# One by one instead of by threes: how the gate matmuls are dealt among the work of attention

## The chip, the cores and the metric

The kernel runs on one core of a Trainium2 chip. The metric is the device time of one execution in microseconds; of several executions the median is given. TensorE (PE) multiplies matrices and accumulates the products in banks of PSUM, VectorE (DVE), ScalarE (ACT) and GpSimd (POOL) work on tiles in SBUF and PSUM, and SyncE (SP) issues most of the DMAs.

## The reference

One layer of a decoder with two token mixers side by side, for 1024 tokens of width 1024, in float32:

```python
h = rmsnorm(x, norm_mix)
(q, kc, vc, ks, vs, kw, vw, nsa_g, rq, rk, rv, rg, gate_a, gate_b) = jnp.split(h @ w_in, offsets, axis=-1)
...                                        # rotary on q, the keys and the retention's q, k
nsa_out = nsa(q, kc, vc, ks, vs, kw, vw, nsa_g, ...)   # 8 heads: compressed + selected + window attention
ret_out = silu(rg) * retention(rq, rk, rv)             # 4 heads of 128, chunks of 128
mix = sigmoid(gate_a) * (nsa_out @ w_proj_a) + sigmoid(gate_b) * (ret_out @ w_proj_b)
x = x + mix @ w_out
h = rmsnorm(x, norm_mlp)
x = x + square(relu(h @ w_up)) @ w_down
return rmsnorm(x, norm_final)
```

The case is about `gate_a` and `gate_b`, the merge gates: two products of the normed input (1024 tokens by 1024) with 1024 x 1024 of weights each, which nobody needs before the two mixers are merged. A query block of 128 tokens selects up to 16 blocks of 64 keys; with 1024 tokens that is all of them, so the selected branch of the kernel runs over all keys up to the query block.

## The kernel before

**Precision.** Every float32 product is made of three: each operand is split into a high part (a cast to the type that TensorE takes, on ScalarE) and a low part (the difference, on VectorE), and high x high, high x low and low x high are accumulated in one PSUM bank. The names end in h and l: `bh`, `bl` are the normed input, `wh`, `wl` a block of weights, `ph`, `pl` the transposed probabilities, `QQ`, `ql` the queries. Nearly all matmuls go through the helper `mm`, so that most rows of TensorE in the profile carry line 156; they are told apart by the tile they write.

**Stages.** From 0 to some 361 us into the profiled execution the input is normed and projected and retention runs; from 362 to 754 us attention; then what is left of the gates and the two mixing projections, the output projection, and the MLP up and down. The stage of the change is attention.

**Attention.** It has 32 units: 8 query blocks (7 down to 0) by 2 key groups by 2 pairs of heads. The selected and the window branch have up to 1024 and 640 keys, the compressed branch 64. A unit has two parts. `scores` multiplies queries by keys into banks `S` (pool `psS`, four banks); VectorE adds the mask there and takes the minimum of the negated scores into `mx` (lines 1008 and 1013), ScalarE makes the exponentials `pS` and `pW` from them (line 1017), VectorE the factors `cf` of sums and head gates (lines 1021 and 1022), and GpSimd scales the exponentials by these (line 1029); it also clears a part of `pW` at the start (line 982). `pv` transposes the probabilities on TensorE into banks `pt` (pool `psT`, two banks; lines 1064 and 1065), ScalarE casts them to `ph` (line 1066), VectorE takes the low part `pl` (line 1067), and TensorE multiplies by the values into `O` (pool `psO`, one bank). Every second unit `prep_q` transposes new queries `qt` into a `pt` bank (line 952) and splits them (lines 955 and 956).

**Gates.** There are 32 of them: 8 blocks of 128 columns of each of the two matrices, by 2 halves of the tokens. `gate_pieces(n)` issues gate n: 24 matmuls of 128x512 that accumulate in one PSUM tile `gps`, then a tanh on ScalarE from that tile into `gst` (line 920), and a DMA on SP's queue that stores it (line 921). The tile comes from pool `psO` and has one buffer, so the first matmul of gate n + 1 must wait until the tanh of gate n has read it; from n = 15 on (`GALT`) odd gates take one of the `S` banks instead. The weights of the next gate are loaded and split ahead (`gate_w`; lines 185 and 186). `gate_pieces` is a generator: at each `yield` it stops and the caller goes on with other work. It yields after every third matmul, so that a gate has 8 pieces, the last of which has the tanh and the store.

**The order.** For TensorE the order of instructions is that in which the code issues them (`tc.manual_schedule`); on VectorE, ScalarE and GpSimd a scheduler orders them. Attention gives each piece of work a time in units: `place(it, n, lo, hi)` puts n steps of a generator at even distances between lo and hi,

```python
        def place(it, n, lo, hi):
            for k in range(n):
                todo.append((lo + (hi - lo) * (k + 0.5) / n, len(todo), it))
```

and the list `todo`, sorted by time, is gone through once. Unit n's scores stand from n - 1 + 0.08 to n - 1 + 0.6, its `pv` from n to n + 1.05. Between n - 1 and n stand `GATES[n]` pieces of gates: 16, then 8 in each of 16 units, 6 in each of 12, 7 in each of 4, which is 244 of all 256. The 12 that are left run after attention, in one row (36 matmuls).

Of the kernel before, what the change touches and what calls it, by code (L numbers as in the profile page):

```python
# [109 lines left out]
def hybrid_block(ctx: ExitStack, tc: tile.TileContext, a: dict, out: bass.AP):  # L110
# [44 lines left out]
    def mm(o, w, m, start, stop):  # L155
        T.matmul(o, w, m, start=start, stop=stop)  # L156
# [62 lines left out]
    with ExitStack() as es:  # L219
# [474 lines left out]
        with ExitStack() as e2:  # L694
# [157 lines left out]
            for j in range(NT):  # L852
# [7 lines left out]
                n = tmp.tile([P, 512], F32, name="n", bufs=4)[:, :256]  # L860
# [13 lines left out]
            for i, j in enumerate(reversed(range(NT))):  # L874
# [6 lines left out]
                n = tmp.tile([P, 512], F32, name="n", bufs=4)  # L881
# [15 lines left out]
    def gate_w(i):  # L897
        if i < 16 and i not in gw:
            src, ii = ("w_ga", i) if i < 8 else ("w_gb", i - 8)
            gw[i] = split_w(a[src][:, ii], (KD, P), pool=wring, part=512)  # L900

    def gate_pieces(n):
        pool = gpool["p"]
        i, th = divmod(n, 2)
        dst, ii = (ga_scr, i) if i < 8 else (gb_scr, i - 8)
        ts = slice(th * 512, (th + 1) * 512)
        gate_w(i)
        gate_w(i + 1)
        h, l = gw[i]
        if n % 2 and n >= GALT and gpool["alt"] is not None:  # L910
            ps = gpool["alt"].tile([P, 512], F32, name="gps", tag="S")
        else:
            ps = pool.tile([P, 512], F32, name="gps", bufs=1)
        parts = [(h, k, x) for k in range(KD) for x in (bh, bl)] + [(l, k, bh) for k in range(KD)]
        for m, (w, k, x) in enumerate(parts):
            mm(ps, w[:, k * P:(k + 1) * P], x[:, k, ts], m == 0, m == len(parts) - 1)
            if m % 3 == 2 and m < len(parts) - 1:
                yield
        o = gsp.tile([P, 512], F32, name="gst")
        A.activation(o, ps, AF.Tanh, scale=0.5)  # L920
        nc.sync.dma_start(dst[ii, :, th], o)
        yield
# [3 lines left out]
    def all_gates():  # L926
        for n in range(32):
            yield from gate_pieces(n)

    gate_it = all_gates()  # L930
# [5 lines left out]
    with ExitStack() as e3:  # L936
# [12 lines left out]
        def prep_q(qb, g):  # L949
            tp = psT.tile([P, 4, P], F32, name="pt", tag="pt")  # L950
            for h in range(4):
                T.transpose(tp[:, h], qs[qb, g][:, h], ident)
            QQ = at.tile([P, 4, P], F32R, name="QQ")
            ql = at.tile([P, 4, P], F32R, name="ql")
            A.activation(QQ, tp, AF.Copy)
            V.tensor_sub(ql, tp, QQ)
            qs[qb, g] = (QQ, ql)
            nxt = 2 * (7 - qb) + g + 2
            if nxt < 16:
                load_q(7 - nxt // 2, nxt % 2)  # L960
            yield
# [139 lines left out]
# [3 lines that stand above are left out]
# [10 lines left out]
            place(it, n_pv(qb) - 1, n, n + 1 + V_END)  # L1114
            place(it, 1, n + 1 + V_LAST, n + 1 + V_LAST)
        for n, k in enumerate(GATES):
            place(gate_it, k, n - 1, n)
        next(prep_q(7, 0))
        for ev in sorted(todo, key=lambda v: v[:2]):
            if len(ev) > 3:  # L1120
# [580 lines left out]
```

## Time and profile before

| what | value |
|---|---|
| runs | 1568.26, 1564.6 and 1562.92 us; median 1564.6 |
| the profiled execution | 1563.77 us, of which 1562.0 are the span of its instructions |
| granted TensorE clock | 0.999 on the mean |
| TensorE busy in attention (362 to 754 us) | 385.84 of 392.00 us, 2385 matmuls and transposes |
| TensorE busy outside it | 1156.40 of 1170.0 us |

Times are microseconds from the start of the span. A row of the timeline gives an instruction's start and its length, and in brackets the idle time ahead of it on its engine and what ended that. The lengths of matmuls overlap, since a matmul's start doesn't wait for the end of the one ahead of it, so a matmul's share of the time is the distance between starts. Busy time is given by engine; PEld is the loading of weights into TensorE, beside the matmuls. In the list of waits a row names the waiting operation, the releasing one, and then total us, times and the longest.

### The profile page before, as it was taken

Reading aid. Unit: us, or ns where it says so; the run is one execution under the profiler, and the core shown is the slowest. Engines: PE = TensorE matmul, PEld = TensorE weight load, DVE = VectorE, ACT = ScalarE, POOL = GpSimd, SP = SyncE. Lnnn points to the kernel's source line nnn. Section 1 sums busy time; section 2 is a strip of 40 time slices with the busy share of each in tenths; the row PEclk is TensorE's granted clock in tenths of the full one; section 3 lists DMA queues with packets and bytes.
Section 4 is the critical chain, followed back from the end, with each engine's and each line's share of the span. In section 5 each row is a group of like instructions: output and inputs, shape, how many; then the busy total and the mean of one; then the engine's idle time right before and its main releaser. Section 6 shows DMA issues by size and latency. Waiting matters only on the chain.

```text
span 1562.0 us, 22775 instructions
## 1 busy us (share of the span) xinstructions
PE 1542.2 (99%) x7845; PEld 1293.8 (83%) x7845; DVE 1080.8 (69%) x2237; ACT 730.9 (47%) x1657; POOL 423.6 (27%) x516
## 2 busy tenths in 40 slices
PE   9999999999999999999999999999999999999997
PEld 7788888988888888888888888888888888888886
DVE  6875663765777777776765379877777667876673
ACT  6663553764677776766522234222222244443452
POOL 3120010002333333333000001744455446521320
PEclk9999999999999999999999999999999999999999
DMA  6202111342111112121644332544444597764472
GB/s 227 68 18 65 58 32 26 112 152 78 48 35 55 48 35 61 43 68 55 198 147 153 109 112 91 188 149 152 158 156 148 185 381 242 219 210 124 148 271 87
DMA packets 98900, 191.85 MB, mean 123 GB/s; under 512 B 26632, under 2 KB 30096, under 8 KB 98784
## 3 DMA queue, kind: packets, MB, share of 16 engines
q1 hardware_dynamic: 97008, 185.82, 36.2%
q0 software_dynamic: 944, 2.93, 0.5%
q10 hardware_dynamic: 832, 1.64, 0.3%
q8 instruction: 62, 1.02, 0.3%
q14 instruction: 54, 0.44, 0.1%
HBM read 140.02 MB, written 50.33 MB: 122 GB/s over the span
## 4 chain that ended last, share of the span: by engine, by line
PE 86%; DVE 6%; ACT 3%; issue 2%; POOL 0%; DMA 0%; POOLq 0%; ACTq 0%; DVEq 0%
PE mmu L156 23%; PE mm L156 20%; PE mmd L156 19%; PE gps L156 9%; PE S L156 4%; PE O L156 4%; PE pt L1065 2%; PE pt L1064 2%; ACT pW L1017 1%; PE pO L156 1%; DVE pl L1067 1%; PE pc L156 1%; DVE S L1008 1%; ACT pS L1017 0%; ACT ph L1066 0%
## 5 line engine op out<-in xcount | busy, mean ns | idle before, releaser
L1217 DVE TENSOR_TENSOR wl<-raw,wh 128x1024 fp32r<-128x1024 f32 x121 | 183.7, 1543 | 67.3 <-ACT wh L1216 66.0
L1216 ACT ACTIVATE wh<-raw 128x1024 fp32r<-128x1024 f32 x121 | 125.1, 1056 | 205.4 <-PE mmd L156 127.7
L156 PE MATMUL mmd<-wh 128*128 128x512 f32 x448 | 174.3, 389 | 0.0
L156 PE MATMUL mmd<-wl,wh 128*128 128x512 f32 x448 | 174.3, 389 | 0.0
L156 PE MATMUL mmd<-wh,wl 128*128 128x512 f32 x448 | 174.3, 389 | 0.0
L156 PE MATMUL mm<-wh,bh 128*128 128x512 f32 (+1 forms) x416 | 160.9, 390 | 1.6 <-ACT bh L271 1.0
L156 PE MATMUL mm<-wh,bl 128*128 128x512 f32 (+1 forms) x416 | 155.0, 376 | 0.0
L156 PE MATMUL mm<-wl,bh 128*128 128x512 f32 (+1 forms) x416 | 154.3, 375 | 0.0
L1067 DVE TENSOR_TENSOR pl<-pt,ph 128x512 fp32r<-128x512 f32 (+1 forms) x160 | 103.8, 649 | 35.9 <-ACT ph L1066 33.4
L1066 ACT ACTIVATE ph<-pt 128x512 fp32r<-128x512 f32 (+1 forms) x160 | 90.3, 568 | 55.2 <-PE pt L1065 54.3
L1029 POOL TENSOR_SCALAR pS<-pS,cf 128x512 f32<-128x512 f32 (+7 forms) x80 | 54.6, 688 | 225.7 <-ACT ph L1066 73.8
L1008 DVE CUSTOM_DVE_ANT_0 S<-S,edge_m 128x512 f32<-128x512 f32 (+3 forms) x192 | 100.8, 530 | 13.8 <-PE S L156 11.2
L156 PE MATMUL gps<-bl,wh 128*128 128x512 f32 x256 | 104.1, 407 | 0.0
L156 PE MATMUL gps<-bh,wh 128*128 128x512 f32 x256 | 103.1, 403 | 0.5 <-ACT gst L920 0.5
L1298 POOL TENSOR_TENSOR sf<-raw 128x512 f32<-128x512 f32 x14 | 22.9, 1633 | 294.2 <-DVE wl L1217 294.2
L156 PE MATMUL mmu<-bh,wh 128*128 128x512 f32 x256 | 99.7, 389 | 0.0
L156 PE MATMUL mmu<-bh,wl 128*128 128x512 f32 x256 | 99.6, 389 | 0.0
L156 PE MATMUL mmu<-bl,wh 128*128 128x512 f32 x256 | 99.6, 389 | 0.0
L156 PEld LDWEIGHTS mmd<-wh,wl 128*128 128x128 f32 x448 | 84.1, 188 | 17.6
L156 PEld LDWEIGHTS mmd<-wh 128*128 128x128 f32 x448 | 84.1, 188 | 17.5
L156 PEld LDWEIGHTS mmd<-wl,wh 128*128 128x128 f32 x448 | 84.1, 188 | 17.3
L156 PEld LDWEIGHTS mm<-wh,bl 128*128 128x128 f32 x416 | 78.1, 188 | 15.4 <-DVE bl L286 0.4
(362 smaller groups left out, 4033.9 us busy)
## 6 DMA issues: line engine op xcount, KB each, us to landing
raw<-u_scr SPq DMA_DIRECT2D x56, 512.0 KB, 3.9
raw<-w_down SPq DMA_DIRECT2D x41, 512.0 KB, 4.8
raw<-w_up SPq DMA_DIRECT2D x32, 512.0 KB, 3.6
u_scr<-u SPq DMA_DIRECT2D x59, 256.0 KB, 2.2
u_scr<-s SPq DMA_DIRECT2D x42, 256.0 KB, 2.0
y<-w_down SPq DMA_DIRECT2D x14, 512.0 KB, 8.3
x<-x SPq DMA_DIRECT2D x8, 512.0 KB, 5.6
qt<-q_scr SPq DMA_DIRECT2D x32, 128.0 KB, 2.4
```

The lines of the kernel that those rows point to most:

```text
L156: T.matmul(o, w, m, start=start, stop=stop)
L1008: V.tensor_tensor_reduce(sc, sc, mk, -0.125, BIGPOS, OP.add, OP.min, mx[:, b:b + 1])
L1017: A.activation(o, sc, AF.Exp, bias=mx[:, m:m + 1], scale=-1.0, accum_out=sums[:, b:b + 1])
L1029: G.tensor_scalar(v, v, cf[:, b:b + 1], 1.0, op0=OP.mult, op1=OP.mult)
L1064: T.transpose(tp[:, bi * 2], p0, ident)
L1065: T.transpose(tp[:, bi * 2 + 1], p1, ident)
L1066: A.activation(ph[:, :n], tp[:, :n], AF.Copy)
L1067: V.tensor_sub(pl[:, :n], tp[:, :n], ph[:, :n])
L1216: A.activation(h[:, :n], r, AF.Copy)
L1217: V.tensor_sub(l[:, :n], r, h[:, :n])
L1298: eng.tensor_tensor(F[:, 1], x11, x21, op=OP.subtract)
```

## The change

The generator yields after each matmul instead of each third, and three times as many steps are placed in each unit. A gate so has 24 pieces; the last still holds the last matmul, the tanh and the store. The numbers in `GATES` stay, and so does the number of gate matmuls in each unit.

```diff
--- before.py
+++ after.py
@@ -914,7 +914,7 @@
         parts = [(h, k, x) for k in range(KD) for x in (bh, bl)] + [(l, k, bh) for k in range(KD)]
         for m, (w, k, x) in enumerate(parts):
             mm(ps, w[:, k * P:(k + 1) * P], x[:, k, ts], m == 0, m == len(parts) - 1)
-            if m % 3 == 2 and m < len(parts) - 1:
+            if m < len(parts) - 1:
                 yield
         o = gsp.tile([P, 512], F32, name="gst")
         A.activation(o, ps, AF.Tanh, scale=0.5)
@@ -1114,7 +1114,7 @@
             place(it, n_pv(qb) - 1, n, n + 1 + V_END)
             place(it, 1, n + 1 + V_LAST, n + 1 + V_LAST)
         for n, k in enumerate(GATES):
-            place(gate_it, k, n - 1, n)
+            place(gate_it, 3 * k, n - 1, n)
         next(prep_q(7, 0))
         for ev in sorted(todo, key=lambda v: v[:2]):
             if len(ev) > 3:
```

In TensorE's order all other instructions keep their sequence. The gates' matmuls stood in 230 unbroken runs and stand in 439 now. Of the rows of VectorE, ScalarE and GpSimd some change places too; the order of SP's queue is the same.

TensorE at the end of gate 6, before (`gps_5258` is gate 6, `gps_5463` gate 7; the numbers at the names are counters, and differ a little between the two kernels):

```order
L156 MATMUL gps_5258<-bh_92,wl_4838 128x512 x3
L156 MATMUL O_5232<-pl_5397,Vw_2774 64x256
L156 MATMUL O_5232<-ph_5396,Vw_2774 128x256
L156 MATMUL O_5232<-pl_5397,Vw_2774 64x256
L156 MATMUL O_5232<-ph_5396,Vw_2774 128x256
L1064 MATMUL pt_5448<-ident_98,pS_5265 128x128
L1065 MATMUL pt_5448<-ident_98,pS_5338 128x128
L1064 MATMUL pt_5448<-ident_98,pS_5265 128x128
L1065 MATMUL pt_5448<-ident_98,pS_5338 128x128
L156 MATMUL O_5232<-pl_5416,Vc_2776 64x256
L156 MATMUL O_5232<-ph_5415,Vc_2776 128x256
L156 MATMUL gps_5463<-bh_92,wh_4837 128x512
```

And the same place after the change (`gps_5240` is gate 6, `gps_5447` gate 7):

```order
L156 MATMUL gps_5240<-bh_92,wl_4820 128x512 x2
L156 MATMUL O_5242<-pl_5398,Vw_2774 64x256
L156 MATMUL O_5242<-ph_5397,Vw_2774 128x256
L156 MATMUL O_5242<-pl_5398,Vw_2774 64x256
L156 MATMUL O_5242<-ph_5397,Vw_2774 128x256
L156 MATMUL gps_5447<-bh_92,wh_4819 128x512
L1064 MATMUL pt_5450<-ident_98,pS_5265 128x128
```

The first matmul of the next gate stood behind four transposes and two more multiplications by values, and stands ahead of the transposes now.

TensorE in the unit of gate 4, where the scores of a new head begin, before:

```order
L156 MATMUL S_4866<-KKs_2771,QQ_4599 128x512
L156 MATMUL S_4866<-KKs_2771,ql_4600 128x512
L156 MATMUL gps_4843<-bl_93,wh_4423 128x512
L156 MATMUL gps_4843<-bh_92,wh_4423 128x512
L156 MATMUL gps_4843<-bl_93,wh_4423 128x512
```

And after:

```order
L156 MATMUL gps_4825<-bl_93,wh_4413 128x512
L156 MATMUL S_4867<-KKs_2771,QQ_4600 128x512
L156 MATMUL S_4867<-KKs_2771,ql_4601 128x512
L156 MATMUL gps_4825<-bh_92,wh_4413 128x512
L1064 MATMUL pt_4875<-ident_98,pS_4645 128x128
```

Three gate matmuls stood in a row behind the scores; now one stands ahead of two scores and one behind them.

VectorE in the same unit, before (`mx_4921` is the minimum over one head's scores, `pl` a low part of probabilities that is taken out of a `pt` bank):

```order
L1008 ISA mx_4921 128x1
L1067 TENSOR_TENSOR pl_4950<-pt_4948,ph_4949 128x512
L1013 TENSOR_TENSOR mx_4921<-mx_4921 128x1
L1067 TENSOR_TENSOR pl_4982<-pt_4980,ph_4981 128x512
L1021 TENSOR_TENSOR sums_4920<-sums_4920 128x2
```

And after:

```order
L1008 ISA mx_4921 128x1
L1013 TENSOR_TENSOR mx_4921<-mx_4921 128x1
L1067 TENSOR_TENSOR pl_4951<-pt_4949,ph_4950 128x512
L1021 TENSOR_TENSOR sums_4920<-sums_4920 128x2
L1022 RECIPROCAL cf_4922<-sums_4920 128x3
```

The second operation on the minimum stood behind a low part, and stands ahead of it now.

## The prediction

> **What bounds the kernel now.** I read the page first, then windows over attention, then the waits of TensorE in that stretch, then single gate ends in the timeline. From the page: busy time, granted clock by slice, and the chain that ended last.
>
> ```profile
> span 1562.0 us, 22775 instructions
> PE 1542.2 (99%) x7845; PEld 1293.8 (83%) x7845; DVE 1080.8 (69%) x2237; ACT 730.9 (47%) x1657; POOL 423.6 (27%) x516
> ...
> PEclk9999999999999999999999999999999999999999
> ...
> PE 86%; DVE 6%; ACT 3%; issue 2%; POOL 0%; DMA 0%; POOLq 0%; ACTq 0%; DVEq 0%
> ```
>
> TensorE (PE) is the bound: it leads the chain with 86%, and its clock stands at full in every slice. The window of attention, and then all that PE waited for in it (total us, times, longest):
>
> ```profile
> 362.00:754.00 392.00, 385.84 (x2385) 331.19 (x2384) 287.08 (x1009) 267.63 (x787) 127.92 (x268) 1.00 0.17 52
> ```
>
> ```profile
> PE pt L1065 <- POOL pS L1029: 1.7, 4, 1.0
> PE S L156 <- ACT pS L1017: 1.3, 2, 0.9
> PE O L156 <- DVE pl L1067: 0.8, 2, 0.4
> PE pt L952 <- DVE pl L1067: 0.7, 1, 0.7
> PE S L156 <- DVE ql L956: 0.6, 2, 0.4
> PE gps L156 <- ACT gst L920: 0.5, 2, 0.2
> PE S L156 <- ACT QQ L955: 0.4, 1, 0.4
> ```
>
> In 392 us PE is busy for 385.84 and waits 6.0 us in 14 places. A better order of the same matmuls can win these 6.0 us and no more; a worse one has no floor. The sixth row is the place to watch: a gate's first matmul waits for ScalarE's tanh (gst), because gates 0 to 14 all accumulate in one PSUM bank. (From gate 15 odd gates use a scores' bank, so nothing waits so.)
>
> How long that bank needs from one gate to the next is seen where it already waits, at the end of gate 1 (PE and ACT, start and length):
>
> ```profile
> 377.37 0.39 PE L156 MATMUL gps<-bh,wl 128*128 128x512 f32 x1
> ...
> 377.80 0.60 ACT L920 ACTIVATE gst<-gps 128x512 f32<-128x512 f32 x1 [0.66 <-PE gps L156]
> ...
> 378.45 0.50 PE L156 MATMUL gps<-bh,wh 128*128 128x512 f32 x1 [0.25 <-ACT gst L920]
> ```
>
> From the start of the last matmul to the start of the next gate's first pass 1.08 us, with ScalarE idle and ready: 0.39 for the matmul to end, 0.6 of tanh, the rest handover. At other gate ends that time is filled. The end of gate 13:
>
> ```profile
> 556.12 0.39 PE L156 MATMUL gps<-bh,wl 128*128 128x512 f32 x1
> 556.35 0.28 PE L156 MATMUL O<-pl,Vw 128*64 128x256 f32 x1
> ...
> 556.54 0.60 ACT L920 ACTIVATE gst<-gps 128x512 f32<-128x512 f32 x1
> ...
> 556.83 0.27 PE L1064 MATMUL pt<-ident,pS 128*128 128x128 f32 x1
> ...
> 557.18 0.36 PE L156 MATMUL O<-pl,Vw 128*64 128x256 f32 x1
> ...
> 557.74 0.40 PE L156 MATMUL gps<-bh,wh 128*128 128x512 f32 x1
> ```
>
> Between the two gates stand four O matmuls (556.35 to 556.83, 0.48 us), four transposes (to 557.26 at 0.11 each), and four more O: 1.62 us, which covers the 1.08.
>
> **The change part by part.** No instruction is added or removed. In the order of PE all matmuls but the gates' stand in the same sequence as before; ahead of any of them the count of gate matmuls differs by one at most. What moves is where each gate matmul stands, and with it a few rows of DVE and ACT.
>
> *1. The gate's end.* The first pair of orders above: the next gate's first matmul now stands ahead of the transposes. It waits for the tanh there, and everything behind it on PE waits too. The cover that is left is the four O. This holds at the ends of gates 2 to 13, twelve times. Cost where ScalarE is ready: 1.08 less the matmul's own 0.23 and the 0.48 of O, 0.37 us. Eight ends (2, 4, 6, 8, 10 to 13) are such: 3.0 us. At gate 1 the four transposes leave the gap altogether: 0.44 us more. At gate 0 nothing changes.
>
> At the ends of gates 3, 5, 7 and 9 ScalarE is late; gate 7:
>
> ```profile
> 470.95 0.64 ACT L185 ACTIVATE wh<-raw 128x512 fp32r<-128x512 f32 x1
> ...
> 471.47 0.61 ACT L920 ACTIVATE gst<-gps 128x512 f32<-128x512 f32 x1
> 471.66 0.33 PE L1065 MATMUL pt<-ident,pS 128*128 128x128 f32 x1 [0.23 <-POOL pS L1029]
> ...
> 472.28 0.40 PE L156 MATMUL gps<-bh,wh 128*128 128x512 f32 x1
> ```
>
> A weight split (wh) stands ahead of the tanh, which ends at 472.08. The next gate would start at 472.13, and its matmul (0.23), four transposes (0.44) and two O (0.23) would be through at 473.03. Before, all that and one gate matmul were through at 472.28 + 0.24 = 472.52. So 0.5 us, less than the wait itself, since the transposes' wait for GpSimd falls inside it. Gate 9 alike. At gates 3 and 5 an O waits for DVE in the old order; gate 5:
>
> ```profile
> 440.80 0.61 ACT L920 ACTIVATE gst<-gps 128x512 f32<-128x512 f32 x1
> ```
>
> ```profile
> 441.70 0.33 PE L156 MATMUL O<-pl,Vw 128*64 128x256 f32 x1 [0.38 <-DVE pl L1067]
> ...
> 442.22 0.40 PE L156 MATMUL gps<-bh,wh 128*128 128x512 f32 x1
> 442.46 0.39 PE L156 MATMUL gps<-bl,wh 128*128 128x512 f32 x1
> ```
>
> The tanh ends at 441.41, so the gate matmul, four transposes and four O (0.47) would be through at 441.46 + 0.23 + 0.44 + 0.47 = 442.60, against 442.46: 0.14, and gate 3 near it, 0.2. Together 1.3. Part 1 is 3.0 + 0.44 + 1.3 = **+4.7 us**. Ends: 3.0 if the late four cost nothing and gate 1 neither; 12 x (0.37 + 0.6) + 0.44 = 12.1 if ScalarE comes a split late at all twelve.
>
> *2. More runs.* The matmuls of the gates stand in 230 unbroken runs before and in 439 now. A run of eight is timed where gates stand alone, a run of three among attention's work:
>
> ```profile
> 754.17 1.98 PE L156 MATMUL gps<-bh,wl 128*128 128x512 f32 x8
> 755.99 0.39 PE L156 MATMUL gps<-bh,wh 128*128 128x512 f32 x1
> ```
>
> ```profile
> 376.92 0.85 PE L156 MATMUL gps<-bh,wl 128*128 128x512 f32 x3
> ...
> 377.61 0.27 PE L1064 MATMUL pt<-ident,pS 128*128 128x128 f32 x1
> ```
>
> Eight take 755.99 - 754.17 = 1.82 us, 0.227 each; three take 0.69, 0.23 each, so 0.01 us over for the run. If all of it belongs to breaking a run, 209 more runs cost 2.1 us; if it belongs to company, nothing. I take the middle, **+1.0 us**. [...]
>
> *3. The waits inside units.* With one gate matmul more ahead of it, a late instruction waits 0.23 us less; the second pair of orders shows one such shift, by which one gate matmul stands ahead of two scores (S) and one behind, where three stood behind. The three long waits among the four below each get one more ahead, and so do the two late waits for GpSimd at the end of the stage; the last row below gets one less.
>
> ```profile
> 392.03 0.44 PE L952 MATMUL pt<-ident,qt 128*128 128x128 f32 x2 [0.73 <-DVE pl L1067]
> ```
>
> ```profile
> 576.06 0.36 PE L156 MATMUL S<-KKw,QQ 128*128 128x192 f32 x1 [0.89 <-ACT pS L1017]
> ```
>
> ```profile
> 674.52 0.33 PE L1065 MATMUL pt<-ident,pS 128*128 128x128 f32 x1 [1.02 <-POOL pS L1029]
> ```
>
> ```profile
> 581.61 0.36 PE L156 MATMUL S<-KKw,QQ 128*128 128x192 f32 x1 [0.45 <-ACT pS L1017]
> ```
>
> Five gains less one loss, 4 x 0.23 = 0.9, and 0.4 for waits under 0.2 us that go with them: **-1.3 us**. Ends: -5.5 (all rows of the list but gst) and 0.
>
> *4. DVE and ACT.* The third pair of orders: on DVE the minimum over a head's scores (mx) stood behind a copy out of PSUM (pl), and now stands ahead of it. The exponentials that wait for mx can start a copy earlier, and in exchange one cast (ph) stands behind them on ACT. This comes in the units of gates 3 to 9. I take 0: earlier exponentials make the tanh no later, a later cast makes it so. Ends, by one cast of 0.6 us either way in seven units: -4.2 and +4.2. SP's queue holds the same rows in the same order; each gate's store goes out with its tanh, and no one waits for it in this stage. GpSimd's clears (MEMSET) shift by one scaling; it is busy 127.92 of 392 us, so I cost them at nothing.
>
> Sum: 4.7 + 1.0 - 1.3 + 0 = +4.4 us. On the profiled execution's 1563.8 us (span 1562.0) that gives **1568.2 us**; the median of the three runs shown, 1564.6, is 0.8 above that execution.
>
> **The rivals.** *Dearer gate ends (slower).* If ScalarE comes late at all twelve ends, part 1 is 12.1 and the time 1575.6. For it: part 4 pushes a cast towards the tanh. Against: at eight ends ScalarE is idle or just done when the gate ends. It decides from 0.6 us of delay. 0.10.
>
> *The finer order pays (faster).* If the one gate matmul between S and S keeps PE busy through all waits of the list, and the gate ends hide, 5.5 us go and 1.0 comes: 1559.3. It needs the tanh within the 0.71 us of one matmul and four O; the rows show 1.08. 0.06.
>
> *Nothing moves.* If DVE and GpSimd, given the idle at the gate ends, are never waited for afterwards, the gains there (up to 5.5) meet the 5.7 of parts 1 and 2: 1564.0. For it: at gates 3, 5, 7 and 9 the old waits do fall into the new one. Against: the three longest stand far from any end of gates 2 to 13, or ahead of it. 0.07.
>
> *The clock falls.* More short stops on PE could lower its clock. [...] Here the window with 14 stops stands at 1.00, so 0.01. The eight warm-up matmuls at the start took 3.59 us against 1.98 for the eight gates above; one unit of 392/32 = 12.2 us at that pace costs 12.2 x (3.59/1.98 - 1) = 9.9 us: 1578.
>
> ```profile
> 1.48 3.59 PE L156 MATMUL pS<-warm 128*128 128x512 bf16 x8 [1.48 <-DVE warm L442]
> ```
>
> **How the numbers follow.** My case has 0.76. A measurement of this kernel tells a change from none beyond about 0.3%, 4.7 us. My sum is just under that, so the case splits, 0.42 within and 0.34 slower. With the rivals: same 0.42 + 0.07 + 0.01 of the faster one = 0.50; slower 0.34 + 0.10 + 0.01 = 0.45; faster 0.05. The range reaches down to the rival in which nothing moves, 1564, and up to where half of the delays of the dear case come, 1573; outside lie the far half of that case, the clock and the faster rival.
>
> **What would show it.** Right: the row "PE gps <- ACT gst" grows from 2 times to about 14, and from 0.5 us to some 4 to 6, with the next gate's first matmul 1.08 us or more after the last; "PE pt <- POOL pS" shrinks; windows outside attention stay. Wrong: that row stays at 2, or rows with S, pt or O grow instead.

## The result, and the profile after

The changed kernel takes 1576.02 us (median of four runs, 1575.84 to 1576.95), the kernel before 1563.80 in the same comparison: a ratio of 1.0077, with a 95% interval of 1.0064 to 1.009. It is 12.2 us slower, outside the range forecast (1564 to 1573).

From the page of the profile after: the span, busy times, the clock by slice, and the chain that ended last.

```profile
span 1574.0 us, 22755 instructions
PE 1547.3 (98%) x7845; PEld 1291.5 (82%) x7845; DVE 1088.9 (69%) x2237; ACT 731.2 (46%) x1657; POOL 422.2 (27%) x516
...
PEclk9999999999999999999999999999999999999999
...
PE 84%; DVE 7%; ACT 5%; issue 2%; DMA 1%; POOL 0%; ACTq 0%; POOLq 0%; DVEq 0%
```

The clock has not fallen. DVE and ACT together have 3 points more of the chain and TensorE 2 fewer: TensorE waits for them more. Where: windows that are cut at the start of the first and of the last gate matmul, first of the kernel before, then after (us, length, then busy time and count of PE, PEld, DVE, ACT and POOL, granted clock, DMA).

```profile
0.00:362.32 362.32, 357.81 (x1913) 302.00 (x1914) 235.07 (x616) 198.99 (x530) 39.79 (x87) 1.00 0.26 84
362.32:761.20 398.88, 392.72 (x2415) 336.83 (x2413) 293.52 (x1015) 273.66 (x793) 127.92 (x268) 1.00 0.18 56
761.20:1562.00 800.80, 791.71 (x3522) 655.00 (x3520) 552.20 (x608) 258.23 (x335) 255.85 (x161) 1.00 0.52 174
```

```profile
0.00:362.42 362.42, 357.85 (x1913) 302.12 (x1914) 235.01 (x616) 198.72 (x530) 39.97 (x87) 1.00 0.26 84
362.42:773.25 410.83, 397.74 (x2415) 334.38 (x2414) 295.24 (x1015) 274.52 (x794) 127.71 (x268) 1.00 0.18 54
773.25:1574.00 800.75, 791.71 (x3522) 654.97 (x3520) 558.67 (x608) 257.95 (x335) 254.50 (x161) 1.00 0.52 174
```

All of it lies in the middle window: 410.83 - 398.88 = 11.95 us, with the same 2415 instructions of TensorE. What TensorE waited for there, after:

```profile
PE pt L952 <- DVE pl L1067: 4.0, 4, 1.4
PE gps L156 <- ACT gst L920: 2.9, 11, 0.7
PE S L156 <- ACT pS L1017: 1.9, 3, 1.0
PE pt L1065 <- POOL pS L1029: 1.3, 2, 0.9
PE O L156 <- DVE pl L1067: 0.9, 3, 0.5
```

The second row is the forecast one, with 11 times in place of 2. The first was not forecast: the transposes of new queries (line 952) waited 0.7 us once before, and wait four times and 4.0 us now.

**The gate's end.** Gate 13 after the change (TensorE and ScalarE):

```profile
566.78 0.60 ACT L920 ACTIVATE gst<-gps 128x512 f32<-128x512 f32 x1
...
566.94 0.29 PE L156 MATMUL O<-ph,Vw 128*128 128x256 f32 x1
...
567.43 0.51 PE L156 MATMUL gps<-bh,wh 128*128 128x512 f32 x1 [0.21 <-ACT gst L920]
567.77 0.27 PE L1064 MATMUL pt<-ident,pS 128*128 128x128 f32 x1
```

As the prediction has it, the gate's first matmul stands behind four O and waits for the tanh. The bracket says 0.21 us; from start to start the stop costs more. The last O begins at 566.94, and after an O of 256 columns the next instruction otherwise starts 0.12 later, so 567.43 - 566.94 - 0.12 = 0.37 go. Then the first transpose starts 0.34 after the gate's matmul, where 0.23 is usual: 0.11 more. Together 0.48 for a listed 0.21. The idle time in a bracket is what is left when TensorE's modelled overlap has run out. The Trainium skill, "Perfetto Trace Analysis", section "Tensor Engine Instruction (MATMUL, LD_WEIGHTS)", says that the ends of TensorE's instructions are estimated and not observed; the busy time here agrees, which grew by 5.02 us (392.72 to 397.74) with the same work.

**The query transposes.** The longest of their waits, after, with the rows of ScalarE and VectorE that lead to it from 455 us on (of the three exponentials, the first):

```profile
455.18 0.27 PE L1065 MATMUL pt<-ident,pW 128*128 128x128 f32 x1
...
455.43 0.69 DVE L1067 TENSOR_TENSOR pl<-pt,ph 128x512 fp32r<-128x512 f32 x1 [0.64 <-ACT ph L1066]
...
456.04 0.15 DVE L1013 TENSOR_TENSOR mx<-mx 128x1 f32<-128x1 f32 x1
...
456.28 0.69 ACT L1017 ACTIVATE pW<-S,mx 128x512 f32<-128x512 f32 x1 [0.88 <-DVE mx L1013]
...
457.58 0.88 ACT L1066 ACTIVATE ph<-pt 128x512 fp32r<-128x512 f32 x2
...
458.22 1.02 DVE L1067 TENSOR_TENSOR pl<-pt,ph 128x512 fp32r<-128x512 f32 x2
...
458.97 0.66 PE L952 MATMUL pt<-ident,qt 128*128 128x128 f32 x4 [1.44 <-DVE pl L1067]
```

And the same place before:

```profile
452.15 0.27 PE L1065 MATMUL pt<-ident,pW 128*128 128x128 f32 x1
...
452.34 1.08 ACT L1066 ACTIVATE ph<-pt 128x512 fp32r<-128x512 f32 x2
...
453.79 0.69 DVE L1067 TENSOR_TENSOR pl<-pt,ph 128x512 fp32r<-128x512 f32 x1
453.96 0.69 ACT L1017 ACTIVATE pW<-S,mx 128x512 f32<-128x512 f32 x1 [0.54 <-DVE mx L1013]
...
454.53 0.66 PE L952 MATMUL pt<-ident,qt 128*128 128x128 f32 x4
```

Before, ScalarE cast the transposed probabilities (ph) and only then waited for the minimum mx that the exponentials pW need. After, the exponentials stand first: ScalarE is idle for 0.88 us and then busy with them, while the cast's input has been there since 455.45. It starts at 457.58, 2.1 us later than it could; VectorE's low part follows, the PSUM bank comes free, and TensorE stands for 1.44 us. The turned pair, the sixth cast of a unit and the three exponentials of the next unit's second head, is found in seven units (the second to the eighth). ScalarE takes its instructions in order; the Trainium skill says so of it in "PSUM — Partial Sum Buffer", section "Engine vs sequencer instructions", and the 0.88 us of idle time ahead of a ready cast agrees.

### The profile page after: what moved, and what is told of

The parts are those of the page before. It is cut to its first block, busy times and chain, and to the rows that moved or that the text cites. A ratio compares the mean times of both kernels' runs of the same rounds, so it can differ in the third digit from the quotient of the medians.

```text
span 1574.0 us, 22755 instructions
## 1 busy us (share of the span) xinstructions
PE 1547.3 (98%) x7845; PEld 1291.5 (82%) x7845; DVE 1088.9 (69%) x2237; ACT 731.2 (46%) x1657; POOL 422.2 (27%) x516
## 4 chain that ended last, share of the span: by engine, by line
PE 84%; DVE 7%; ACT 5%; issue 2%; DMA 1%; POOL 0%; ACTq 0%; POOLq 0%; DVEq 0%
PE mmu L156 23%; PE mm L156 19%; PE mmd L156 19%; PE gps L156 9%; PE S L156 4%; PE O L156 3%; PE pt L1065 2%; PE pt L1064 2%; ACT pW L1017 1%; DVE pl L1067 1%; ACT ph L1066 1%; DVE S L1008 1%; PE pO L156 1%; ACT pS L1017 1%; PE pc L156 1%
## 5 line engine op out<-in xcount | busy, mean ns | idle before, releaser
L1217 DVE TENSOR_TENSOR wl<-raw,wh 128x1024 fp32r<-128x1024 f32 x121 | 188.3, 1582 | 64.3 <-ACT wh L1216 62.8
```

The source lines that it names most:

```text
L1217: V.tensor_sub(l[:, :n], r, h[:, :n])
```

## The experiments

Theory: two causes that add, the gate's end on TensorE and the turned pair on ScalarE. The rivals: one of them alone, or the number of runs. All times are medians; the kernel before had 1563.6 to 1564.0 in these comparisons. Line numbers in the rows of experiments are shifted by the lines that they add.

### 1: the changed kernel with ScalarE's old order

Issue order alone, without a wait, is pinned: each of the three exponentials stands behind the cast. (`us` is the list of the units' records, `u["n"]` a unit's number from 0.) TensorE's order stays as it was in the changed kernel. On ScalarE the seven casts move and, with one of them, a weight split (wh); on VectorE the low parts behind the casts move, and a few small rows beside them.

```diff
-                        A.activation(o, sc, AF.Exp, ...)
+                        e = A.activation(o, sc, AF.Exp, ...)
+                        if i and base == 2:
+                            u.setdefault("late", []).append(e.ins)
...
-                A.activation(ph[:, :n], tp[:, :n], AF.Copy)
+                c = A.activation(ph[:, :n], tp[:, :n], AF.Copy)
+                if b0 == 10 and 1 <= u["n"] <= 7:
+                    for e in us[u["n"] + 1]["late"]:
+                        tc.add_manual_dep(e, c.ins.name, NOSYNC, reason="order")
```

> The changed kernel, one by one everywhere, with one thing of the old order put back: in the seven units of qb 7 and 6 after the first, the sixth cast ph stands ahead of the three exponentials pW on ScalarE again. Theory (two causes that add: gate ends +5.6 us, this order on ScalarE +4 to +5, the rest +1 to +2): about 1571.5 us (1570 to 1573), the wait of the query transposes for DVE (PE pt L952 <- DVE pl) falls from 4.0 us to 1 or less, and the wait for gst stays at some 11 times and 3 us. Rival 1 (those waits come from TensorE's own order, not from ScalarE's): 1576, waits as in the changed kernel. Rival 2 (one cause, each is born of the stop at the gate's end): 1576 as well.

1571.62 us, ratio to the kernel before 1.0047 (1.0033 to 1.0061). From its waits:

```profile
PE gps L156 <- ACT gst L920: 3.6, 14, 0.7
...
PE pt L952 <- DVE pl L1072: 0.6, 1, 0.6
```

The long waits of the query transposes went with ScalarE's order, on an unchanged order of TensorE: the first rival falls, and so does the second, that they come from the gates' ends, of which there are more here than before (14).

### 2: the kernel before with the turned order on ScalarE

The list `late` is filled as in the first experiment.

```diff
+                if b0 == 10 and 1 <= u["n"] <= 7:
+                    tc.add_manual_dep(c.ins, us[u["n"] + 1]["late"][-1].name, NOSYNC, reason="order")
```

> The kernel before, gates by threes, with only that order on ScalarE turned: in the same seven units the three exponentials pW stand ahead of the sixth cast ph. Theory: 1563.8 + 4 to 5 = 1568.3 us (1567 to 1570), the query transposes wait some 4 us for DVE at four places, the wait for gst stays at 2 times and 0.5 us. Rival (the order on ScalarE hurts only where the gates are dealt finely, since three gate matmuls in a row cover it): 1564.

1571.79 us, 1.005 (1.0037 to 1.0062). From its waits:

```profile
PE pt L952 <- DVE pl L1071: 6.2, 4, 2.1
PE O L156 <- DVE pl L1071: 2.2, 4, 0.7
...
PE gps L156 <- ACT gst L920: 0.5, 2, 0.3
```

The turned pair alone costs 7.9 us, not 4 to 5: the expectation was too low. Its five runs lie far apart (1570.16 to 1574.77), but the window of attention in its profiled execution says the same: 406.80 us against 398.88. The likely reason, argued and not shown, is that without stops at the gates' ends TensorE reaches the transposes earlier and waits longer for them; and O waits for low parts, 2.2 us in place of 0.8. TensorE's order is that of the kernel before; on ScalarE four weight splits changed places with the casts, so the pair is not quite alone.

### 3 and 4: the edges of a gate and its middle, apart

Of the 24 matmuls of a gate, the third experiment leaves the first three and the last three together at their old times and deals the eighteen between one by one; the fourth does the reverse.

```diff
+            if m == 0:
+                yield
             mm(ps, w[:, k * P:(k + 1) * P], x[:, k, ts], m == 0, m == len(parts) - 1)
-            if m < len(parts) - 1:
+            for _ in range(2 if m in (2, 20) else 1 if 3 <= m < 20 else 0):
                 yield
...
         yield
+        yield
```

> Gates dealt one by one, but the first three and the last three matmuls of each gate stay together at their old times, so that the distance from one gate's last matmul to the next gate's first is the old one. ScalarE keeps the changed order. Theory: 1576.0 - 5.6 = 1570.4 us (1569 to 1572), wait for gst back at 2 times and 0.5 us, query transposes still wait some 4 us for DVE. Rival 1 (the gate's end is the single cause): 1564. Rival 2 (dealing finely costs by the number of runs): 1574 or more.

```diff
+            mid = 3 <= m < 21
+            if mid and m % 3 == 0:
+                yield
             mm(ps, w[:, k * P:(k + 1) * P], x[:, k, ts], m == 0, m == len(parts) - 1)
-            if m < len(parts) - 1:
+            for _ in range(2 * (m % 3 == 2) if mid else m < 23):
                 yield
```

> The reverse: the first three and the last three matmuls of each gate are dealt one by one as in the changed kernel, the eighteen between them by threes as before. ScalarE's order is the old one but for one unit. Theory: 1563.8 + 5.6 = 1569.4 us (1568 to 1571), wait for gst at some 11 times and 3 us, query transposes wait 1 us or less for DVE. Rival 1 (the fine order between the ends is the cause): 1564. Rival 2 (the stops at the gates' ends cause the rest): 1575 or more.

The third: 1570.25 us, 1.0037 (1.0025 to 1.005). The fourth: 1571.40 us, 1.0048 (1.0035 to 1.0061). From the waits of the third and of the fourth:

```profile
PE pt L955 <- DVE pl L1070: 5.1, 4, 1.9
...
PE gps L156 <- ACT gst L922: 0.5, 2, 0.3
```

```profile
PE gps L156 <- ACT gst L923: 5.1, 14, 0.8
...
PE pt L955 <- DVE pl L1070: 0.5, 1, 0.5
```

Each shows one wait without the other. So the middle, dealt one by one, turns ScalarE's order (the pair is turned in all seven units of the third kernel, in one of the fourth), and the edges bring the stops at the gates' ends. The fourth costs 7.5 us, 2 more than expected: at the ends of gates 3, 5, 7 and 9 a weight split stands ahead of the tanh, as in the kernel before, and the new wait there is 0.4 to 0.8 us in place of 0.2. In the first experiment the weight splits stand earlier, and these four ends wait 0.2 us like the others.

### 5: both taken out

The edits of the third and the first together: the middle one by one, edges and ScalarE's pair as before.

> Both causes taken out together: the first three and the last three matmuls of a gate at their old times, the eighteen between them one by one, and the sixth cast ph ahead of the exponentials pW on ScalarE. Theory (the two causes are all there is; dealing finely costs and gains next to nothing): 1563.9 us, between 1562.5 and 1565.5, waits of TensorE as in the kernel before, about 6 us. Rival 1 (more unbroken runs cost by themselves, the prediction's +1.0 to 2.1): 1565 to 1566 with no more waits than before. Rival 2 (the finer order pays once its two costs are gone): 1561 or less.

1563.92 us, 1.0002 (0.9994 to 1.0011), as expected. With that the four corners are there:

| | pair as before | pair turned |
|---|---|---|
| edges as before | 1563.8 (by threes), 1563.9 (middle by ones) | 1571.8 (by threes), 1570.25 (middle by ones) |
| edges by ones | 1571.4 (middle by threes), 1571.6 (by ones) | 1576.0 (by ones, the changed kernel) |

The edges cost 7.5 to 7.8 us with the old pair, the pair 6.4 to 7.9 with the old edges, and both 12.2, less than their sum of some 14 to 16. The likely reason is that who stops at a gate's end is later at the query transposes and waits less there: the row of their wait lists 4.0 us in the changed kernel and 5.1 in the third. Along a cell the grain of the middle makes 0.1 to 1.5 us. The kernel with 1571.4 has the pair turned in one of the seven units.

The runs of one kernel differ mostly ahead of attention. In the profiled executions the first gate matmul starts at 361.85 to 365.38 us, while what follows the start of the last one takes 800.78 to 800.83 us in every kernel. The window between the two is the cleaner measure: 398.88 us before, 399.03 in experiment 5, 405.99 in 1, 406.34 in 4, 404.95 in 3, 406.80 in 2 and 410.83 in the changed kernel. By it the edges cost 7.0 to 7.5 us, the pair 5.9 to 7.9, and both 11.95.

### 6, 7 and 8: another bank for odd gates

The wait for the tanh can also be taken away by a second bank: `GALT = 1` in place of 15, so that odd gates use a bank of the scores from gate 1 on. Experiment 6 does it in the kernel of experiment 1, 7 in the kernel before, 8 in the changed kernel.

> The changed kernel, one by one at the gates' ends too, with the old order on ScalarE as in the first experiment, and odd gates in a bank of the scores from gate 1 on (GALT = 1), so that no gate has to wait for the tanh of the one ahead of it. Theory: the wait for gst falls from 14 times to 1 or 0 and 1571.6 - 6 to 7 = 1565 us (1563.5 to 1566.5). Rival (a bank less for the scores brings a new wait of S for ScalarE or DVE): 1568 or more.

> The kernel before with odd gates in a bank of the scores from gate 1 on: the control for the bank alone. Theory (the bank is not missed): 1563.2 us (the 0.5 us of the two waits for gst go), 1562.5 to 1564.5. Rival (a bank less for the scores costs something): 1565 or more.

> The changed kernel with odd gates in a bank of the scores from gate 1 on, and ScalarE's order left as the change made it. It takes the wait at the gates' ends away by another means than the third experiment did. Theory: about what the third experiment gave, 1570 us (1569 to 1572): the wait for gst gone, the query transposes waiting some 5 us for DVE. Rival (the third experiment was saved by the old times of the gates' edges, not by the wait for gst that went): 1574 or more.

1574.65 us (1.0068, 1.0054 to 1.0082), 1567.93 us (1.0026, 1.0016 to 1.0036) and 1578.83 us (1.0097, 1.0084 to 1.0111). All three expectations failed, and the rival of 6 and 7 came. The time of 8 lies where its rival put it as well, but the cost of the bank is in it, so it doesn't show that rival. From the waits of 6 and of 7:

```profile
PE S L156 <- ACT pS L1017: 8.3, 12, 1.1
```

```profile
PE S L156 <- ACT pS L1017: 4.8, 9, 0.9
```

The row for gst is gone in both, and the scores, with three banks in place of four while an odd gate accumulates, wait for the exponentials to read theirs. In the control that makes 4.3 us. These times can't tell, then, what the gates' ends cost; from 7 to 6 the finer order still adds 6.7 us, though neither has a wait for gst. The traces show where it lies. Counted from start to start, the stops at the gates' ends, 7.3 us in experiment 1, are gone in 6, and the scores' stops for the exponentials grow from 3.0 to 14.5 us (8.9 in 7). Most of them stand inside an odd gate, ahead of its eighth or fifteenth matmul, and not at a gate's end. The longest of experiment 6 is ahead of the eighth matmul of gate 7:

```profile
465.10 0.36 PE L156 MATMUL S<-KKw,QQ 128*128 128x192 f32 x1 [1.05 <-ACT pS L1017]
```

So it is another wait than the one at the gates' ends; why the finer order makes it longer where a bank is missing stays open. And 8 less 6, 4.2 us, is the price of the turned pair once more, beside 4.4 us between the changed kernel and experiment 1.

### 9 and 10: what the waits pointed to

If the bank is dear, take it later; and if the pair is dear, set it right where the kernel before has it turned too, in the first unit.

```diff
-GALT = 15
+GALT = 19
...
+                if b0 == 10 and u["n"] <= 7:
```

Experiment 9 is the kernel before with this and the rest of the first experiment's edit; experiment 10 is the kernel of experiment 5 with this.

> The kernel before, by threes, with two small things that the earlier runs pointed to: the sixth cast ph stands ahead of the exponentials pW in the first unit too (it didn't in the kernel before), and odd gates take a bank of the scores only from gate 19 on, not from 15. TensorE's order is the old one. Theory: the query transposes' wait of 0.7 us (0.9 with the restart) and the two waits of S for pS of 1.3 us (1.7 with the restarts) go, 1563.7 - 2.6 = 1561.1 us (1560 to 1562.5). Rival (they come back as other waits, or gates 16 to 18 wait for the tanh): 1563 to 1565.

> The same two things in the kernel of the fifth experiment, in which the eighteen middle matmuls of a gate are dealt one by one. Theory (dealing finely is worth nothing either way, and the waits go): 1563.9 - 1.3 - 1.65 = 1561 us, within 1 us of the kernel by threes with the same two things. Rival 1 (finer pays where its costs are gone): 1559.5 or less. Rival 2 (the waits come back elsewhere): 1563 to 1565.

1560.82 us (0.9979, 0.997 to 0.9988) and 1560.64 us (0.9977, 0.9969 to 0.9986): both faster than the kernel before and the changed one. The two edits were not run apart. The waits of the query transposes and of S for pS are gone from experiment 9; its longest row left:

```profile
PE pt L1067 <- POOL pS L1031: 1.5, 3, 1.0
```

With both costs out, one by one (in the middle of a gate) and by threes are 0.2 us apart, less than the comparison can tell: the finer order brings nothing that shows even there.

## Why the prediction was wrong

**Part 4, DVE and ACT, is the step that failed.** It saw the exchange (exponentials earlier, a cast behind them), took 0, and bounded it by one cast of 0.6 us in seven units, 4.2 us. Alone it costs 6.4 to 7.9 us. A cast that is put behind others is late by all that stands ahead of it, and by what that waits for: 0.88 us of idle time and three exponentials, 2.1 us in the rows above. And the prediction looked at whom the exponentials serve, not at whom the cast serves: a PSUM bank that TensorE needs next. In the changed kernel its share is about 4 us: reckoned from start to start over all of attention (each distance between two starts less what it is where nothing waits), the query transposes' stops went from 1.1 to 5.0 us, and taking the turned pair away gave 4.4 (4.8 in the window of attention). That the bound of 4.2 comes near this is luck: it counted a cast's length in seven units, and the loss sits in four waits of the query transposes, three of them new.

**Part 1, the gates' ends**, had the mechanism right. Reckoned in the same way, it is +5.1 us in the changed kernel, less than half of the loss, against the 4.7 forecast. The eight ready ends cost 4.1 in place of 3.0, mostly since 0.11 us of restart behind each was left out (at gate 11 ScalarE was late, too); gate 1 cost 0.43 against 0.44, and the late four 0.6 against 1.3, after the old waits that fell into them. By themselves, with ScalarE's old order, the gates' ends are dearer: 7.5 to 7.8 us, or 7.0 to 7.5 in the window of attention. The forecast of the row was half right: 11 times where some 14 were named, and 2.9 us where 4 to 6 were, because the row shows only the idle part of a stop.

**Part 3, the waits inside units**, was to give back 1.3 us. In the changed kernel the other stops grew by 1.7 (with 5.1 and 4.0 that is 10.8 of the 11.95 us; 1.2 are spread too thinly to be laid to one). In experiment 5 they shrank by 0.9 in that reckoning, so there may be a small gain, and only there: the time does not show it.

**Part 2, more runs**, took +1.0 us. In experiment 5 these other stops shrink by 0.9 us and the time stays (1.0002), which leaves about that much for the runs; but this is a difference within what the comparison can tell, and that more runs cost nothing isn't excluded.

Against the sum of +4.4 us the window of attention grew by 7.6 more: 3.9 of it are part 4, 3.0 part 3 (a loss of 1.7 in place of a gain of 1.3), 0.4 part 1, and the rest is spread. So part 3 is the second term that failed, and its cause is not separated. Two smaller slips: the ceiling of "these 6.0 us and no more" counts listed idle time, while from start to start the stops of the kernel before hold some 10 us; and half of the dear case's 7.4 us on top of 1568.2 is 1571.9, not 1573. Neither would have taken the range to 1576.0.

**The rivals.** The dear case gave 1575.6 us, and 1576.0 was measured, but not by its mechanism: ScalarE was not a split late at all twelve ends, and the ends alone give 1571.6. That nothing moves holds for the kernel of experiment 5; that the finer order pays holds for none, since 10 is within 0.2 us of 9. The granted clock stood at 1.00 in all three windows.

What stays open: why the scheduler turned the pair. Experiments 3 and 4 show that it does so in all seven units where the eighteen middle matmuls are dealt one by one, and in one where they are not; they do not show what in its reckoning does it.

## What to carry to other kernels

When an order written by hand for one engine moves, look at what a scheduler then does to the others, pair by pair, and price each turned pair by the wait that now stands ahead of the later one, and by who needs its bank, not by its own length. Where a buffer passes from one group of work to the next, the last and the first instruction of the groups want their distance; the grain between them hardly matters here, as long as the scores have their four banks. Separate two suspected causes by the four corners, since each alone may cost more than its share of the sum.

## What the hardware showed beyond that

A stop of TensorE costs more than the idle time listed for it: 0.48 us from start to start for 0.21 listed, 0.11 of it in a slower start of the instruction behind. And a bank taken from four that the scores turn over cost 4.3 us, though it served only every second gate (experiment 7).
